# A two-layer decoder trunk: queries and keys multiplied with both parts of x^T in one operand, and the first attention's 1/rms moved into its tanh

## The chip, the cores and the metric

The kernel runs on one core of one Trainium2 chip. The metric is device time in microseconds for one execution of the whole program (two layers). PE is the matrix engine, ACT the scalar engine, DVE the vector engine, POOL the general one; SP issues the loads.

## The reference

The input x is 256 tokens by 1024. Both layers do the following, all in float32:

```python
h = _rmsnorm(x, g_mix)
proj = h @ w_in                     # q,k,v of three attentions, gates, an indexer
br_a = stick_breaking(qa, ka, va)   # 8 heads of 64, no positions
br_b = forgetting(qb, kb, vb)       # softmax with a forget bias
br_c = indexed_sparse(qc, kc, vc)   # top 64 keys for each query, by an indexer
y = sum(sigmoid(gate) * (br @ w_branch))
x = x + y @ w_out
x = x + relu(rmsnorm(x) @ w_up)**2 @ w_down
```

In the first attention, with z = q·k/8, a weight is sigmoid(z) times the product of 1 - sigmoid over the keys that lie between; the kernel takes sigmoid(z) from tanh(z/2).

## The kernel before

**Split operands.** Each float32 operand goes to PE as two parts, a rounded one ("hi") and the rest ("lo"), and a product is three matmuls: hi·hi, hi·lo, lo·hi (`mm3`, lines L119, L120, L121). The weights are split on the chip: a load brings 1 MB into `raw`, and for each half of it ACT copies the hi part (`whi`, L91) and DVE subtracts (`wlo`, L92, 128x1024). There are four buffers of `whi` and four of `wlo`, so the fifth half after a given one is not split before PE has done with that one. x^T stands in `xT` tiles that hold the hi and lo parts of two blocks of 128 features side by side; 1/rms of a token is not in it and is multiplied in later.

**One `feat`.** Queries and keys of the two attentions without positions are made by `feat`, eight times in each layer (`qa`, `ka`, `qb`, `kb`, two column groups each). A call takes 256 weight columns as two blocks b of 128. For each block and each of 8 blocks k of features there are three matmuls with the weights as the stationary operand and 256 columns of x^T moving; both blocks share one PSUM tile `mm`. DVE then multiplies the tile by `rb`, 1/rms laid along the tokens (L500, 128x512, `full`), and `q_stack` (ACT L145, DVE L147) or `k_stack` (ACT L153, L156, L157, DVE L155) splits `full` into the operands of the scores. There are three buffers of `mm` and four of the group "w3" that `full`, `e`, `th`, `m` and `R` share.

**Order of the work in a layer.** First the columns of the sparse attention, then `qa` and `ka` for two column groups, the values `va`, and beside them the indexer: its scores `sc` (L363 on ACT, L365 on DVE), then the search for the 64 best, 8 rounds of a maximum (L372) and a replacement (L373) on DVE for each 128 queries. Behind the values comes a first gate projection (its 8 k-blocks for one half of the tokens in a row, so that it takes four halves of weights in some 5 us), then the softmax of the sparse attention (`zc`, `e` L475, `pT` L440, `pTl` L444, `av` L456, `avs` L463) beside `qb` and `kb`, then the first attention (`za`, `th` L605, a scan `R` L617). The up projection of the feed-forward part, later in the layer, already moves both parts of x^T at once (`up_mm`, L686 with 512 columns, L687 with 256) and adds the halves (L674, L675).

Each engine runs its own instructions strictly in an order that a scheduler fixes when the program is built, from the dependences and its own estimate of times; so an edit in one place also shifts instructions of others.

Of the kernel before, what the change touches and what calls it, by code (L numbers as in the profile page):

```python
# [12 lines left out]
AF = mybir.ActivationFunctionType  # L13
OP = mybir.AluOpType

T, D, DEPTH, COLS, DFF = 256, 1024, 2, 7244, 4096
# [16 lines left out]
def trunk_kernel(ctx: ExitStack, tc: tile.TileContext, x, positions, g_mix, w_in, b_forget, w_branch,  # L33
                 w_out, g_mlp, w_up, w_down, g_final, out):
    nc = tc.nc
    act, dve, pool, pe, dma = nc.scalar, nc.vector, nc.gpsimd, nc.tensor, nc.sync
# [7 lines left out]
    def mm_tile(name="mm"):  # L44
        return ps.tile([128, 512], F32, name=name, tag="mm", bufs=3)
# [65 lines left out]
    def w_cols(src, off, rs):  # L111

        raw = raw_tile(8, 256)
        dma.dma_start(raw, AP(src, off, [[rs, 128], [128 * rs, 8], [1, 256]]))
        return [split(raw[:, :, 128 * b:128 * b + 128], 8, 128) for b in range(2)]

    def mm3(o, a, b, start, stop):
        (ah, al), (bh, bl) = a, b
        pe.matmul(o, ah, bh, start=start, stop=False)  # L119
        pe.matmul(o, ah, bl, start=False, stop=False)  # L120
        pe.matmul(o, al, bh, start=False, stop=stop)  # L121
# [9 lines left out]
    def blk(tiles, k, c0=0, c1=256, p0=0, p1=128):  # L131
        h, l = tiles[k // 2][:2]
        return h[p0:p1, k % 2, c0:c1], l[p0:p1, k % 2, c0:c1]
# [83 lines left out]
    for layer in range(DEPTH):  # L217
        wi0 = layer * D * COLS
        if layer == 0:
            wfirst = w_rows(w_in, C0 + 736, COLS, 0, 364, loads=4)  # L220
            load_x(1)
            xt, ss, part = norm_in(0, (at_tile, pt_tile))
# [3 lines left out]
        with tc.tile_pool(name=f"att{layer}", bufs=1, reuse_waits="tile") as att:  # L226
# [5 lines left out]
            rb = small.tile([128, 272], F32, name="rb", tag="rb", bufs=1)[:, 0:256]  # L232
            act.activation(rb, rp[:, 0:256], AF.Copy)

            rhalf = small.tile([128, 2], F32, name="rhalf", tag="rhalf", bufs=1)
# [101 lines left out]
            for n, c in enumerate((KI, KC, KC + 64)):  # L337
# [3 lines left out]
                p = at_tile("kT")  # L341
# [15 lines left out]
            for j, c, n in SEG:  # L357
                for h in range(4):
                    z = at_tile("zi")
                    i = h % 2  # L360
# [71 lines left out]
            ctok = small.tile([128, 2, NH], F32, name="ctok", tag="ctok", bufs=1)  # L432
            dve.tensor_copy(ctok, p[:, 0:16].rearrange("p (j h) -> p j h", j=2))


            def p_parts(e, i, scale):

# [52 lines left out]
                                           op0=OP.mult, op1=OP.mult)  # L490
                return e

            def feat(off, cp, is_q):

                o = mm_tile()
                for b, (h, l) in enumerate(w_cols(w_in, wi0 + off + cp * 256, COLS)):
                    for k in range(8):
                        mm3(o[:, b * 256:b * 256 + 256], (h[:, k, :], l[:, k, :]), blk(xt, k), k == 0, k == 7)
                full = work.tile([128, 2, 256], F32, name="full", tag="w3", bufs=4)
                dve.tensor_mul(full, o.rearrange("p (b t) -> p b t", b=2), rb.unsqueeze(1).to_broadcast([128, 2, 256]))  # L500
                if is_q:
                    q = stacked("qs")
                    q_stack(q, full, 0.125)
                    return q
                kt = stacked("ks")
                lo = att.tile([128, 2, 2, 256], F32R, name="ksl", tag="q4", bufs=8)
                k_stack(kt, lo, full)
                return kt, lo
# [21 lines left out]

            qa, ka = [], []
            for cp in range(2):
                qa.append(feat(0, cp, True))
                ka.append(feat(512, cp, False))
            va = values(1024)


# [62 lines left out]
            for b in range(4):  # L600
                th = work.tile([128, 2, 384], F32, name="th", tag="w3", bufs=4)
                for i in range(2):
                    z = at_tile("za")
                    qk(z, qa, ka, b, i)
                    act.activation(th[:, i, :], z[:, 0:384], AF.Tanh, scale=0.5)  # L605
                for c in (0, 256):
                    v = th[:, :, c:c + 128]
                    pool.affine_select(v, v, [[0, 2], [-1, 128]], OP.is_gt, -1.0, base=0, channel_multiplier=1)

                m = work.tile([128, 768], F32, name="m", tag="w3", bufs=4)  # L610
                pool.tensor_scalar(m[:, 0:767], th.rearrange("p i s -> p (i s)")[:, 1:768], -0.5, 0.5,
                                   op0=OP.mult, op1=OP.add)
                m2 = m.rearrange("p (i s) -> p i s", i=2)
                pool.memset(m2[:, :, 127:128], 0.0)
                pool.memset(m2[:, :, 383:384], 0.0)
                R = work.tile([128, 768], F32, name="R", tag="w3", bufs=4)
                dve.tensor_tensor_scan(R[:, ::-1], m[:, ::-1], ends[:, ::-1], 0.0, op0=OP.mult, op1=OP.add)  # L617
                dve.scalar_tensor_tensor(R, th.rearrange("p i s -> p (i s)"), 1.0, R, op0=OP.add, op1=OP.mult)
                Rv = R.rearrange("p (i s) -> p i s", i=2)
                parts = [p_parts(Rv, i, 0.5) for i in range(2)]  # L620
                av_pair(parts, lambda i, s: va[:, s, 2 * b + i, :], blk(brA, b))
# [45 lines left out]
        with tc.tile_pool(name=f"mlp{layer}", bufs=1, reuse_waits="tile") as mlp:  # L667
# [11 lines left out]
                act.activation(hi, r3, AF.Copy)  # L679
                dve.tensor_sub(lo, r3, hi.bitcast(F32))  # L680

            def up_mm(o, wb, ks):

                h, l = wb
                for k in ks:
                    pe.matmul(o, h[:, k, :], xt[k // 2][2][:, :, k % 2, :], start=k == 0, stop=False)  # L686
                    pe.matmul(o[:, 256:512], l[:, k, :], blk(xt, k)[0], start=False, stop=k == 7)  # L687

            first = []
            for c in range(16):  # L690
                uT.append((mlp.tile([128, 2, 256], F32R, name=f"uh{c}"), mlp.tile([128, 2, 256], F32R, name=f"ul{c}")))
# [67 lines left out]
```

## Time and profile before

| | |
|---|---|
| median of 3 runs | 885.59 us (885.42 to 887.14) |
| the profiled execution: its time | 883.07 us |
| its span in the trace | 881.3 us |
| PE, DVE, ACT, POOL busy | 98%, 73%, 61%, 13% of the span |
| granted clock of PE, mean | 0.997 of full speed |
| from layer 0 to the same place of layer 1 | about 432 us |

A share of busy time is a mean over the whole span. Matmuls are pipelined: the duration shown for one is longer than the distance to the next, and it is the distance from start to start that fills the time. On DVE and ACT too the next instruction can start slightly before the end shown of the one ahead of it.

### The profile page before, as it was taken

How to read it: one execution, taken by the hardware profiler on the slowest of the kernel's cores; microseconds unless marked ns; L12 is line 12 of the kernel's file. 1: busy time of each engine (PE TensorE's matmuls, PEld its weight loads, DVE VectorE, ACT ScalarE, POOL GpSimd, SP SyncE). 2: the span in 40 equal slices, each digit the busy share in tenths (PEclk: the TensorE clock that was granted, in tenths of full speed). 3: DMA queues.
4: the chain of work that ended last, by engine and by line, in shares of the span. 5: the costliest groups of instructions: out<-in, count | busy, mean ns of one | idle time of the engine just before them, and what ended most of it. 6: DMA issues, size and time to landing. Idle time of an engine off the chain costs nothing.

```text
span 881.3 us, 12928 instructions
## 1 busy us (share of the span) xinstructions
PE 865.4 (98%) x4830; PEld 759.2 (86%) x4830; DVE 645.0 (73%) x1072; ACT 533.4 (61%) x902; POOL 114.3 (13%) x216
## 2 busy tenths in 40 slices
PE   7999999999999999999999999999999999999996
PEld 6998998888888888888899989988888888888884
DVE  5889787978767777545468987789777587775552
ACT  6766886676466555435366758677755665554432
POOL 2300422234001000000011014022610100000001
PEclk9999999999999999999999999999999999999998
DMA  8744544344565555555466363454246566555521
GB/s 295 246 144 144 191 145 144 128 158 145 191 191 166 179 187 190 190 195 185 148 201 202 131 202 133 144 186 131 97 161 220 185 191 192 191 191 191 191 97 48
DMA packets 102479, 150.91 MB, mean 171 GB/s; under 512 B 2928, under 2 KB 58256, under 8 KB 102416
## 3 DMA queue, kind: packets, MB, share of 16 engines
q1 hardware_dynamic: 102416, 150.08, 52.2%
q8 instruction: 38, 0.62, 0.3%
q14 instruction: 25, 0.20, 0.1%
HBM read 149.02 MB, written 1.05 MB: 170 GB/s over the span
## 4 chain that ended last, share of the span: by engine, by line
PE 92%; DVE 5%; ACT 1%; DMA 1%; issue 1%; SPq 0%; POOL 0%; POOLq 0%; ACTq 0%
PE mm L120 20%; PE mm L119 20%; PE mm L121 20%; PE mm L686 13%; PE mm L687 6%; PE av L456 2%; PE pT L440 2%; PE at L120 1%; PE at L121 1%; PE at L119 1%; DVE wlo L92 1%; DVE qs L147 1%; PE xtp L170 1%; ACT qs L145 1%; DMA x<-in_x_dram 1%
## 5 line engine op out<-in xcount | busy, mean ns | idle before, releaser
L92 DVE TENSOR_TENSOR wlo<-raw,whi 128x1024 fp32r<-128x1024 f32 (+3 forms) x289 | 347.9, 1207 | 167.9 <-ACT whi L91 165.8
L91 ACT ACTIVATE whi<-raw 128x1024 fp32r<-128x1024 f32 (+3 forms) x289 | 298.8, 1037 | 240.0 <-PE mm L121 135.9
L686 PE MATMUL mm<-xT,whi 128*128 128x512 f32 x496 | 173.3, 393 | 0.6 <-DVE ut L675 0.6
L687 PE MATMUL mm<-xT,wlo 128*128 128x256 f32 x496 | 139.0, 280 | 0.0
L120 PE MATMUL mm<-wlo,xT 128*128 128x512 f32 (+2 forms) x320 | 122.1, 382 | 0.5 <-DVE wlo L92 0.5
L121 PE MATMUL mm<-whi,xT 128*128 128x512 f32 (+2 forms) x320 | 121.1, 381 | 0.0
L119 PE MATMUL mm<-whi,xT 128*128 128x512 f32 (+2 forms) x320 | 118.5, 381 | 0.4 <-ACT xT L175 0.4
L686 PEld LDWEIGHTS mm<-xT,whi 128*128 128x128 f32 x496 | 92.8, 187 | 21.9 <-PE mm L687 1.1
L121 PE MATMUL mm<-whi,ul 128*128 128x512 f32 x256 | 99.7, 390 | 0.0
L120 PE MATMUL mm<-wlo,uh 128*128 128x512 f32 x256 | 99.7, 389 | 0.0
L119 PE MATMUL mm<-whi,uh 128*128 128x512 f32 x256 | 98.9, 389 | 0.0
L687 PEld LDWEIGHTS mm<-xT,wlo 128*128 128x128 f32 x496 | 93.7, 189 | 0.1
L121 PE MATMUL mm<-xT,wlo 128*128 128x256 f32 x256 | 73.6, 287 | 0.0
L119 PE MATMUL mm<-xT,whi 128*128 128x256 f32 x256 | 73.2, 286 | 0.0
L120 PE MATMUL mm<-xT,whi 128*128 128x256 f32 x256 | 73.2, 286 | 0.0
L120 PEld LDWEIGHTS mm<-wlo,xT 128*128 128x128 f32 x320 | 60.4, 189 | 10.4 <-DVE wlo L92 1.4
L119 PEld LDWEIGHTS mm<-whi,xT 128*128 128x128 f32 x320 | 60.3, 189 | 10.3 <-ACT xT L175 0.8
L121 PEld LDWEIGHTS mm<-whi,xT 128*128 128x128 f32 x320 | 60.3, 189 | 9.1
L187 POOL TENSOR_TENSOR ms<-ss 128x2 f32<-128x2 f32 (+1 forms) x6 | 4.3, 718 | 469.4 <-ACT junk L180 295.2
L119 PEld LDWEIGHTS mm<-whi,uh 128*128 128x128 f32 x256 | 48.1, 188 | 10.0
L121 PEld LDWEIGHTS mm<-whi,ul 128*128 128x128 f32 x256 | 48.0, 188 | 10.0
L120 PEld LDWEIGHTS mm<-wlo,uh 128*128 128x128 f32 x256 | 48.1, 188 | 9.8
(218 smaller groups left out, 1487.9 us busy)
## 6 DMA issues: line engine op xcount, KB each, us to landing
raw<-in_w_in_dram SPq DMA_DIRECT2D x48, 1024.0 KB, 5.0
raw<-in_w_up_dram SPq DMA_DIRECT2D x32, 1024.0 KB, 5.1
raw<-in_w_down_dram SPq DMA_DIRECT2D x32, 1024.0 KB, 4.9
raw<-in_w_branch_dram SPq DMA_DIRECT2D x12, 1024.0 KB, 4.9
raw<-in_w_out_dram SPq DMA_DIRECT2D x8, 1024.0 KB, 4.9
raw<-in_w_in_dram SPq DMA_DIRECT2D x8, 736.0 KB, 5.2
raw<-in_w_in_dram SPq DMA_DIRECT2D x3, 728.0 KB, 4.3
out_dram<-x SPq DMA_DIRECT2D x4, 256.0 KB, 2.2
```

What stands on the lines that cost most here:

```text
L91: act.activation(h3[:, i:i + m], raw[:, i:i + m], AF.Copy)
L92: dve.tensor_sub(l3[:, i:i + m], raw[:, i:i + m], h3[:, i:i + m].bitcast(F32))
L119: pe.matmul(o, ah, bh, start=start, stop=False)
L120: pe.matmul(o, ah, bl, start=False, stop=False)
L121: pe.matmul(o, al, bh, start=False, stop=stop)
L145: act.activation(dst[half(i), :, i, :], src[half(i)], AF.Copy, scale=scale)
L147: dve.scalar_tensor_tensor(dst[half(1 - i), :, i, :], src[half(i)], scale, dst[half(i), :, i, :].bitcast(F32), op0=OP.mult, op1=OP.subtract)
L170: pe.transpose(p[:, i * 256 + j * 128:i * 256 + j * 128 + 128], xs[j][h][:, c:c + 128], ident)
L440: pe.transpose(p[:, q * 128:q * 128 + 128], e[:, i, q * 128:q * 128 + 128], ident)
L456: pe.matmul(o[:, c + c0:c + 256], v, p[:, a:b], start=s == 0 and n == 0, stop=s == 1 and n == 1)
L686: pe.matmul(o, h[:, k, :], xt[k // 2][2][:, :, k % 2, :], start=k == 0, stop=False)
L687: pe.matmul(o[:, 256:512], l[:, k, :], blk(xt, k)[0], start=False, stop=k == 7)
```

## The change

`feat` gets two switches. With `wide`, each block b has a PSUM tile of its own, and each k takes two matmuls: the hi weights against hi and lo of x^T side by side (512 columns, L439), and the lo weights against hi (256 columns, L440), added into the second half of the tile. ACT copies the second half to `full` (L509), and DVE adds the first half (L510). With `scaled`, DVE multiplies by 1/rms as before (L519). `qa` is wide and not scaled; `ka` is scaled and not wide, as before; `qb` and `kb` are both. Since `qa` now lacks its 1/rms, the tanh of the first attention multiplies by `rhalf` (half of 1/rms of the query's token, which is a row there); it is cut in two, for the two 128-query parts. `up_mm` is only moved up in the file.

```diff
+            def up_mm(o, wb, ks):
+
+                h, l = wb
+                for k in ks:
+                    pe.matmul(o, h[:, k, :], xt[k // 2][2][:, :, k % 2, :], start=k == 0, stop=False)
+                    pe.matmul(o[:, 256:512], l[:, k, :], blk(xt, k)[0], start=False, stop=k == 7)
...
-            def feat(off, cp, is_q):
-
-                o = mm_tile()
-                for b, (h, l) in enumerate(w_cols(w_in, wi0 + off + cp * 256, COLS)):
-                    for k in range(8):
-                        mm3(o[:, b * 256:b * 256 + 256], (h[:, k, :], l[:, k, :]), blk(xt, k), k == 0, k == 7)
+            def feat(off, cp, is_q, wide=True, scaled=True):
+
+
                 full = work.tile([128, 2, 256], F32, name="full", tag="w3", bufs=4)
-                dve.tensor_mul(full, o.rearrange("p (b t) -> p b t", b=2), rb.unsqueeze(1).to_broadcast([128, 2, 256]))
+                ws = w_cols(w_in, wi0 + off + cp * 256, COLS)
+                if wide:
+                    for b, (h, l) in enumerate(ws):
+                        o = mm_tile()
+                        up_mm(o, (h, l), range(8))
+                        act.activation(full[:, b], o[:, 256:512], AF.Copy)
+                        dve.tensor_add(full[:, b], o[:, 0:256], full[:, b])
+                    src = full
+                else:
...
+                if scaled:
+                    dve.tensor_mul(full, src, rb.unsqueeze(1).to_broadcast([128, 2, 256]))
...
-                qa.append(feat(0, cp, True))
-                ka.append(feat(512, cp, False))
+                qa.append(feat(0, cp, True, scaled=False))
+                ka.append(feat(512, cp, False, wide=False))
...
-                    act.activation(th[:, i, :], z[:, 0:384], AF.Tanh, scale=0.5)
+                    for j, c, n in SEG:
+                        act.activation(th[:, i, c:c + n], z[:, c:c + n], AF.Tanh, scale=rhalf[:, j:j + 1])
```

Numbers behind an underscore below are the program's own numbers of tiles; a tile that both programs have may carry different ones.

**First place: PE at the first `qa` block of layer 0.** Before, three matmuls of 256 columns for each k:

```order
L119 MATMUL mm_665<-xT_103,whi_668 128x256
L120 MATMUL mm_665<-xT_103,whi_668 128x256
L121 MATMUL mm_665<-xT_103,wlo_669 128x256
L119 MATMUL mm_665<-xT_103,whi_668 128x256
L120 MATMUL mm_665<-xT_103,whi_668 128x256
L121 MATMUL mm_665<-xT_103,wlo_669 128x256
L119 MATMUL mm_665<-xT_104,whi_668 128x256
L120 MATMUL mm_665<-xT_104,whi_668 128x256
L121 MATMUL mm_665<-xT_104,wlo_669 128x256
```
With the change, two for each k, of 512 and 256 columns:

```order
L439 MATMUL mm_676<-xT_103,whi_668 128x512
L440 MATMUL mm_676<-xT_103,wlo_669 128x256
L439 MATMUL mm_676<-xT_103,whi_668 128x512
L440 MATMUL mm_676<-xT_103,wlo_669 128x256
L439 MATMUL mm_676<-xT_104,whi_668 128x512
L440 MATMUL mm_676<-xT_104,wlo_669 128x256
```
What moved: nine instructions have become six, with as many moving columns.

**Second place: DVE in layer 0, behind the values' last weights.** Before: `wlo_983` are the last weights of `va`, `wlo_1271` the first of the gate behind it; `qs` and `ksl` are the split queries and keys, `sc` and `m8` the search:

```order
L147 SCALAR_TENSOR_TENSOR qs_726<-full_724,qs_726 64x2x256
L155 TENSOR_TENSOR ksl_793<-full_790,ks_792 64x2x256 x2
L373 MATCH_REPLACE sc_492<-m8_559,sc_492 128x128
L92 TENSOR_TENSOR wlo_983<-raw_976,whi_982 128x1024
L147 SCALAR_TENSOR_TENSOR qs_863<-full_861,qs_863 64x2x256 x2
L372 MAX m8_562<-sc_492 128x8
L372 MAX m8_565<-sc_492 128x8
L92 TENSOR_TENSOR wlo_1271<-raw_1268,whi_1270 128x1024
L433 COPY ctok_663<-cumt_659 128x16
L423 CAST crow_654<-chi_652 128x256
L373 MATCH_REPLACE sc_492<-m8_562,sc_492 128x128
```
With the change the last weights of `va` are `wlo_959` (six rows further up), and `wlo_1247` and `wlo_1251` are the first two halves of the gate:

```order
L92 TENSOR_TENSOR wlo_1247<-raw_1244,whi_1246 128x1024
L373 MATCH_REPLACE sc_492<-m8_553,sc_492 128x128
L372 MAX m8_556<-sc_492 128x8
L373 MATCH_REPLACE sc_492<-m8_556,sc_492 128x128
L372 MAX m8_559<-sc_492 128x8
L373 MATCH_REPLACE sc_492<-m8_559,sc_492 128x128
L147 SCALAR_TENSOR_TENSOR qs_612<-ctT_607,qs_612 64x2x256 x2
L372 MAX m8_562<-sc_492 128x8
L372 MAX m8_565<-sc_492 128x8
L147 SCALAR_TENSOR_TENSOR qs_714<-full_665,qs_714 64x2x256 x2
L155 TENSOR_TENSOR ksl_781<-full_719,ks_780 64x2x256
L373 MATCH_REPLACE sc_492<-m8_562,sc_492 128x128
```
What moved: rounds of the search that stood ahead of the values' weights now stand between the gate's weights. From behind the third of the four halves of `va` to the last half of the gate, in layer 0, DVE has 7 replacements of 128 columns where it had 3, 6 maxima of 128 where it had 3, 3 score rows L365 of 256 columns where it had none, one cast less (L427), and all else alike; PE has six more matmuls (`zi`, 256 columns). In layer 1 the same stretch has 5 and 5 of the 128-column steps, one step less of each kind of 256, 2 score rows, and four more `zi`.

**Third place: PE and DVE in layer 1, in the sparse attention's softmax.** Before, PE behind the last scores `zc` of the stage; the rows go on with matmuls of `kb`, 53 of them in all before the first use of `pTl_5434`:

```order
L350 MATMUL zc_5527<-kl_4785,qs_4929 128x256
L456 MATMUL av_5384<-pTl_5381,vc_4934 128x256
L456 MATMUL av_5384<-pTh_5380,vc_4934 128x128
L456 MATMUL av_5384<-pTl_5381,vc_4934 128x128
L119 MATMUL mm_5795<-xT_3920,whi_5798 128x256
L120 MATMUL mm_5795<-xT_3920,whi_5798 128x256
L440 MATMUL pT_5429<-ident_76,e_5410 128x128
L121 MATMUL mm_5795<-xT_3920,wlo_5799 128x256
L119 MATMUL mm_5795<-xT_3920,whi_5798 128x256
L120 MATMUL mm_5795<-xT_3920,whi_5798 128x256
```
DVE before, in the same place, up to that `pTl`:

```order
L155 TENSOR_TENSOR ksl_5247<-full_5244,ks_5246 64x2x256 x2
L475 ISA e_5532,mx_5533<-zc_5527,mb_4906 128x128
L475 ISA mx_5533 128x1
L475 ISA e_5532,mx_5533<-zc_5527,mb_4906 128x256
L475 ISA mx_5533 128x1
L92 TENSOR_TENSOR wlo_5874<-raw_5867,whi_5873 128x1024
L463 TENSOR_TENSOR avs_5393<-av_5384,avs_5393 64x256 x2
L500 TENSOR_TENSOR full_5788<-mm_5729,rb_4532 128x512
L444 SCALAR_TENSOR_TENSOR pTl_5434<-pT_5429,pTh_5433 128x384
```
With the change PE has there, behind `zc_5443`, the transposes and eight matmuls of the first attention's scores (`za`), and then at once the matmuls that need `pTl_5350`:

```order
L447 MATMUL pT_5345<-ident_76,e_5326 128x128 x2
L447 MATMUL pT_5353<-ident_76,e_5326 128x128 x3
L349 MATMUL za_5957<-ks_5037,qs_4971 128x128
L350 MATMUL za_5957<-ksl_5038,qs_4971 128x128
L349 MATMUL za_5957<-ks_5037,qs_4971 128x256
L350 MATMUL za_5957<-ksl_5038,qs_4971 128x256
L349 MATMUL za_5964<-ks_5037,qs_4971 128x128
L350 MATMUL za_5964<-ksl_5038,qs_4971 128x128
L349 MATMUL za_5964<-ks_5037,qs_4971 128x256
L350 MATMUL za_5964<-ksl_5038,qs_4971 128x256
L463 MATMUL av_5361<-pTh_5349,vc_4874 128x256
L463 MATMUL av_5361<-pTl_5350,vc_4874 128x256
```
DVE with the change:

```order
L155 TENSOR_TENSOR ksl_5163<-full_5101,ks_5162 64x2x256 x2
L493 RECIPROCAL rs_5391<-sm_5389 128x4
L482 ISA e_5448,mx_5449<-zc_5443,mb_4846 128x128
L482 ISA mx_5449 128x1
L482 ISA e_5448,mx_5449<-zc_5443,mb_4846 128x256
L482 ISA mx_5449 128x1
L92 TENSOR_TENSOR wlo_5819<-raw_5816,whi_5818 128x1024
L470 TENSOR_TENSOR avs_5309<-av_5300,avs_5309 64x256 x2
L451 SCALAR_TENSOR_TENSOR pTl_5350<-pT_5345,pTh_5349 128x384
L451 SCALAR_TENSOR_TENSOR pTl_5358<-pT_5353,pTh_5357 128x384
```
What moved: the first attention's scores come earlier, and 53 matmuls of `kb` no longer lie between the last scores of the stage and the first use of the `pTl` that stands behind them on DVE.

## Rows read from the trace of the kernel before

**Rows 1.** The page: busy time by engine, and the chain that ended last by engine.

```profile
PE 865.4 (98%) x4830; PEld 759.2 (86%) x4830; DVE 645.0 (73%) x1072; ACT 533.4 (61%) x902; POOL 114.3 (13%) x216
...
PE 92%; DVE 5%; ACT 1%; DMA 1%; issue 1%; SPq 0%; POOL 0%; POOLq 0%; ACTq 0%
```

**Rows 2.** What PE waited for: us in total, times, longest.

```profile
PE av L456 <- DVE pTl L444: 0.6, 2, 0.3
...
PE mm L120 <- DVE wlo L92: 0.5, 2, 0.3
```

**Rows 3.** Timeline of PE, inside a block of `feat`: start, duration (us), instruction.

```profile
38.64 0.28 PE L119 MATMUL mm<-xT,whi 128*128 128x256 f32 x1
...
39.00 0.28 PE L119 MATMUL mm<-xT,whi 128*128 128x256 f32 x1
```

**Rows 4.** Timeline of PE, the up projection.

```profile
299.91 0.39 PE L686 MATMUL mm<-xT,whi 128*128 128x512 f32 x1
...
305.81 0.39 PE L686 MATMUL mm<-xT,whi 128*128 128x512 f32 x1
```

**Rows 5.** DVE by line and shape: count, busy us, mean ns of one, idle before.

```profile
L92 DVE TENSOR_TENSOR wlo<-raw,whi 128x1024 fp32r<-128x1024 f32 x264 | 325.9, 1237 | 152.3 <-ACT whi L91 150.5
L675 DVE TENSOR_TENSOR ut<-mm,ut 128x256 f32<-128x256 f32 x62 | 25.8, 418 | 0.0
...
L444 DVE SCALAR_TENSOR_TENSOR pTl<-pT,pTh 128x384 fp32r<-128x384 f32 x48 | 25.3, 551 | 1.0 <-ACT pTh L443 0.7
L463 DVE TENSOR_TENSOR avs<-av,avs 64x256 f32<-64x256 f32 x48 | 20.1, 419 | 7.8 <-ACT avs L461 7.4
...
L155 DVE TENSOR_TENSOR ksl<-full,ks 64x512 fp32r<-64x512 f32 x16 | 11.5, 719 | 0.8 <-PE zc L349 0.4
L500 DVE TENSOR_TENSOR full<-mm,rb 128x512 f32<-128x512 f32 x16 | 11.0, 687 | 0.3
...
L475 DVE CUSTOM_DVE_ANT_0 e<-zc,mb 128x256 f32<-128x256 f32 x16 | 6.6, 420 | 0.0
...
L372 DVE MAX8 m<-sc 128x8 f32<-128x128 f32 x16 | 4.7, 293 | 0.3
...
L373 DVE MATCH_REPLACE8 sc<-m,sc 128x128 f32<-128x128 f32 x16 | 4.4, 278 | 0.0
L475 DVE CUSTOM_DVE_ANT_0 e<-zc,mb 128x128 f32<-128x128 f32 x16 | 4.4, 287 | 0.5 <-POOL mb L377 0.4
...
L365 DVE SCALAR_TENSOR_TENSOR sc<-ri,wh,sc 128x256 f32<-128x256 f32 x6 | 2.8, 472 | 0.0
L373 DVE MATCH_VALUE_LOAD sc<-m,sc 128x8 f32 x32 | 2.8, 88 | 0.5
```

**Rows 6.** ACT by line and shape, the same columns.

```profile
L674 ACT ACTIVATE ut<-mm 128x256 f32<-128x256 f32 x62 | 22.3, 363 | 0.0
...
L605 ACT ACTIVATE th<-za 128x384 f32<-128x384 f32 x16 | 7.2, 487 | 9.0 <-DVE R L617 4.5 <-PE za L350 4.4
```

**Rows 7.** Timeline of DVE, the end of `va` and the gate, layer 0.

```profile
59.00 1.23 DVE L92 TENSOR_TENSOR wlo<-raw,whi 128x1024 fp32r<-128x1024 f32 x1 [0.29 <-ACT whi L91]
...
78.25 1.22 DVE L92 TENSOR_TENSOR wlo<-raw,whi 128x1024 fp32r<-128x1024 f32 x1
```

**Rows 8.** Timeline of PE, the gate's last weights, layer 0.

```profile
78.64 0.39 PE L121 MATMUL mm<-whi,xT 128*128 128x512 f32 x1
78.87 0.39 PE L119 MATMUL mm<-whi,xT 128*128 128x512 f32 x1
79.52 0.50 PE L120 MATMUL mm<-wlo,xT 128*128 128x512 f32 x1 [0.26 <-DVE wlo L92]
```

**Rows 9.** Timeline of PE, eight score matmuls and the next instruction.

```profile
96.70 0.22 PE L349 MATMUL zc<-kh,qs 128*128 128x128 f32 x1
...
97.61 0.40 PE L120 MATMUL mm<-wlo,xT 128*128 128x512 f32 x1
```

**Rows 10.** Window 100 to 131 us: busy (count) of PE, PEld, DVE, ACT, POOL; clock; DMA.

```profile
100.00:131.00 31.00, 31.00 (x257) 30.72 (x256) 26.43 (x55) 27.43 (x62) 10.14 (x15) 1.00 0.42 137
```

More of the change, by code (lines that the diff above doesn't have):

```diff
@@ L491, in softmax_pair @@
                 return e
-            def feat(off, cp, is_q):
-                o = mm_tile()
-                for b, (h, l) in enumerate(w_cols(w_in, wi0 + off + cp * 256, COLS)):
-                    for k in range(8):
-                        mm3(o[:, b * 256:b * 256 + 256], (h[:, k, :], l[:, k, :]), blk(xt, k), k == 0, k == 7)
-                full = work.tile([128, 2, 256], F32, name="full", tag="w3", bufs=4)
-                dve.tensor_mul(full, o.rearrange("p (b t) -> p b t", b=2), rb.unsqueeze(1).to_broadcast([128, 2, 256]))
+            def feat(off, cp, is_q, wide=True, scaled=True):
+                full = work.tile([128, 2, 256], F32, name="full", tag="w3", bufs=4)
+                ws = w_cols(w_in, wi0 + off + cp * 256, COLS)
[7 more added lines that the diff above has]
+                else:
+                    o = mm_tile()
+                    for b, (h, l) in enumerate(ws):
+                        for k in range(8):
+                            mm3(o[:, b * 256:b * 256 + 256], (h[:, k, :], l[:, k, :]), blk(xt, k), k == 0, k == 7)
+                    src = o.rearrange("p (b t) -> p b t", b=2)
+                if scaled:
+                    dve.tensor_mul(full, src, rb.unsqueeze(1).to_broadcast([128, 2, 256]))
                 if is_q:
@@ L680, in up_done @@
                 dve.tensor_sub(lo, r3, hi.bitcast(F32))
[L682 to L687, printed above, removed]
             first = []
```

## The prediction

> **What bounds the kernel now.** I read the page first. PE is busy for 98% of the span, and the chain that ended last runs through PE for 92% of it [rows 1]; the clock is granted in full where it is listed [rows 10]. So the time is the sum of the distances between matmuls, plus what PE waits. The list of PE's waits is next: inside the layers it has hardly any, 0.5 to 0.6 us in two pieces each [rows 2]. Two consequences. What the change takes from PE's own work is saved, unless a wait takes its place; and there is almost no wait left that the change could remove, but many that it could create, since DVE is busy for 73% of the span and ACT for 61%. So the third look is at the places where PE waits already. The `wlo` wait is at the last weights of the first gate: PE starts a matmul at 78.87 and the next, which needs them, at 79.52 instead of 0.23 later (78.64 to 78.87), 0.42 us late [rows 8]. They were made from 78.25 to 79.47 [rows 7], and DVE had no idle time between the end of the `wlo` that starts at 59.00 and this one: 19.24 us of queue. Of that stretch PE has nothing to spare; it will show every DVE instruction that is put into it. The second such place is the softmax beside `qb` and `kb`: from 100 to 131 us ACT is busy 27.43 of 31 us and DVE 26.43 [rows 10], while PE never stops.
>
> **The change on PE.** For each k of a block three matmuls become two, with the same columns. Three take 0.36 us (38.64 to 39.00) [rows 3]. The pair has run in the up projection: 17 of them from 299.91 to 305.81, 0.347 us each [rows 4]. That is 0.013 us less. Six of the eight `feat` calls in a layer are wide, so 6 calls x 2 blocks x 8 k x 2 layers = 192 groups: 2.5 us. The starts are printed to 0.01 us, so 0.36 may be 0.355 to 0.365, and the gain 1.5 to 3.5 us; I take 2.5. No gain at all is excluded by these rows, since both forms ran here, on operands of the same kind. A rule weighed against this: the Trainium skill, "TensorE: Matmul & The Clock Gate", section "Wait — 56ns, not 53.3ns?", gives a warm matmul a fixed cost of about 2.5 ns beyond its columns. By that figure the 192 matmuls less would give only 0.5 us, and the whole sum would end 2 us higher; the rows show 13 ns for each, and the sum goes by them.
>
> **The change on ACT and DVE, by work.** Each of the 24 wide blocks adds an ACT copy and a DVE add, both seen in the up projection at 0.363 and 0.418 us [rows 5, 6]: 8.7 and 10.0 us in all. Four multiplications of `qa` go, at 0.687 [rows 5]: 2.7 us. With `qb` and `kb` the multiplication now reads SBUF rather than PSUM; no row shows it, and I keep 0.687 (at best it falls to that of an add of half the size, 0.42; at worst it takes two of them, 0.84; 8 of them change 2 us of DVE's work either way, none of it in the stretch of [rows 7]). The tanh: 16 of 0.487 become 32; the second one costs ACT between nothing and another 0.363 each, 0 to 5.8 us, in a stage where ACT waited 9.0 us ahead of this line [rows 6]: nothing for PE. Behind PE's saving there is thus more work of the helpers, some 4 to 7 us for each layer on either engine, and over the whole run there are gaps enough; what counts is which queues it lengthens.
>
> **First wait: the gate behind the values.** The order shows that the helper work of `qa` pushes rounds of the indexer's search to later places: in layer 0, between the third half of `va`'s weights and the last half of the gate's, DVE has four replacements of 128 columns more (0.278 and a load of 0.088 each), three maxima (0.293) and three score rows (0.472) [rows 5]: 1.46 + 0.88 + 1.42 = 3.8 us, less a small cast, which I put at 0.2 by estimate: 3.5. PE gets six `zi` matmuls more in the same stretch, at 0.114 (eight such from 96.70 to 97.61) [rows 9]: 0.7. The stretch starts on both sides at the same event, since the third half can be split only when PE has left the `ka` block whose buffer it takes. As DVE is already 0.42 late there, all of the difference shows: 2.8 us. Bounds: nothing if ACT's or the load's lateness was what set DVE in this stretch (then DVE would have shown idle time, it shows 0.29 at the start only), 3.5 if PE's `zi` are hidden. In layer 1 the same count is 2 x (0.366 + 0.293 + 0.472) = 2.3, less one maximum and one replacement of 256 columns and the cast (1.1, estimated from the 128-column rows times 1.4, and 0.2), less 4 `zi` (0.5): 0.7. What is behind the late `wlo` on DVE is the rest of the search, for which nobody waits yet. Together 3.5.
>
> **Second wait: `pTl_5350` in layer 1.** From the end of the scores `zc_5438` DVE has, until this `pTl` is there: two pairs of `e` (0.42 + 0.287 each), `ksl` twice (0.719), a `wlo` (1.237), `avs` twice (0.419) and the `pTl` (0.551) [rows 5]: 5.5 us. PE has 27 small matmuls in that time (`av`, `zc`, `pT`, `za`): at 0.114, 3.1 us [rows 9]. So PE would wait 2.4 us. Before, 53 matmuls of `kb`, at 0.12 [rows 3], stood in between, 6 us more, and PE waited for nothing. Bounds: 0, if `ksl` and the first pair are through earlier than I count; 2.4. I take 2.2, since DVE starts an instruction slightly before the shown end of the one ahead. Behind it stand `pTl_5358` (0.551) and the add that frees a PSUM tile for the next `kb` block (0.418), 1.0 us, while PE has 13 small matmuls, 1.5 us: no third wait there.
>
> **Sum.** -2.5 + 3.5 + 2.2 = +3.2 us. The profiled execution took 883.07, its span 881.3; the median of the runs is 885.59, 2.5 above it. The change is put on the median: 888.8 us, where a profiled execution would show about 886.3.
>
> **The rivals.** *Faster.* The queues catch up: in the stage of `qa` DVE's own work rises by only 4 x 0.418 - 2 x 0.687 = 0.3 us per layer, and the search that stands later could find DVE free later. Then both waits stay where they were, at tenths, and 2.5 us are saved: 883.1. For it speaks that DVE idled for 152 us ahead of `wlo` over the run [rows 5], against it that none of this idle time lies in the stretch of [rows 7]. It decides if DVE enters the gate's stretch more than 3 us ahead. The Trainium skill, "Perfetto Trace Analysis", section "Identifying the Most-Contended Engine", would have the engine of highest occupancy improved first, which PE is here; by that rule alone the time is this rival's. *No change.* One of the two places costs what I count, the other little: -2.5 + 2.2 to 3.5 = about 0 to +1, 885.3 to 886.6. *Slower still.* From 100 to 131 us ACT gets 8 copies per layer, 2.9 us on 27.4 of 31 [rows 6, 10], and the tanh of the first attention now falls into the same time with `za` moved up. Above 31 the scan `R` and the transposes behind it come late too: 2 us a layer, 892.8.
>
> **How the numbers follow.** A measurement of this kernel can tell about 0.2%, 1.8 us, from no change. My forecast, 887.4 to 890.5, has a chance of 0.36, the slower rival 0.17, so slower 0.53; no change 0.27; faster 0.20. The forecast's time is the likeliest: 888.8. The range reaches down to the faster rival's upper part, 883.5, and up to 892.0, leaving about 0.15 below and 0.05 above.
>
> **What the new profile would show.** Right: L439 and L440 at a pair pitch of 0.347; a wait of PE for `wlo` of some 3 us around 79 us and of 1 us at the same place of layer 1; a wait for `pTl` of 2 us near the end of the sparse attention in layer 1; PE's busy time 2 to 3 us lower. Wrong: PE's waits as short as before, or long waits at other names (`full`, `whi`, `R`, a PSUM tile held by the new adds), or a pair in `feat` slower than in the up projection.

## The result and the profile after

The changed kernel takes **897.4 us** (895.97 to 898.52, 4 runs) against 885.5 us (883.97 to 887.14, 4 runs) in the same comparison: a ratio of 1.0125, 95% interval [1.011, 1.0139]. It is slower, as forecast, but by 11.9 us instead of 3.2, and outside the range.

First two lines of the page of the changed kernel (busy time by engine; the chain that ended last), which answer to [rows 1]:

```profile
PE 870.6 (97%) x4638; PEld 750.9 (84%) x4638; DVE 653.0 (73%) x1092; ACT 542.4 (61%) x942; POOL 115.1 (13%) x216
...
PE 85%; DVE 9%; issue 2%; ACT 2%; POOL 1%; DMA 1%; SPq 0%; POOLq 0%; DVEq 0%; ACTq 0%
```

And its list of what PE waited for (us in total, times, longest), which answers to [rows 2]:

```profile
PE mm L120 <- DVE wlo L92: 4.6, 5, 1.2
...
PE za L349 <- DVE mx L482: 1.8, 2, 1.4
PE pT L447 <- DVE R L638: 1.7, 2, 1.2
PE av L463 <- ACT full L509: 1.3, 1, 1.3
PE mm L439 <- DVE ut L695: 0.6, 2, 0.3
PE zc L349 <- DVE ctok L433: 0.4, 1, 0.4
```

The chain has gone from 92% PE to 85%, and the waits inside the layers from some 2 us to over 10, under names that hardly waited before: weights (`wlo`), scores (`za`), the scan's transposes (`pT`), a value matmul (`av`). The idle time in this list is counted from the modelled end of the matmul ahead; the distance from start to start, less the usual one, is longer, and it is what the span pays. By that measure:

| place | layer 0 | layer 1 | before |
|---|---|---|---|
| gate behind the values (78 to 83, 520 us) | 2.4 | 1.1 | 0.4 each |
| softmax of the sparse attention (116 to 117, 552 to 554 us) | 2.3 | 2.4 | about 0 |
| scan R and its transposes (146, 603 us) | 1.3 | 0.8 | 0 |
| weights and values behind the next R (172, 608 to 611 us) | 1.3 | 1.9 | 0 |

That is 12.7 us more than before, less what the pairs save. From the first `rp` matmul at a layer's start to the first `xtp` transpose behind its attentions, layer 0 grew by 6.45 us (244.82 to 251.27) and layer 1 by 4.67 (244.36 to 249.03), 11.1 together. The table less 2.1 us of saving gives 10.6; two waits of 0.5 us at `av` that the kernel before had (199 and 631 us) are gone as well, so some 1.5 us lie in pieces that the table doesn't list. The two profiled spans differ by 13.8 us, and the other 2.7 lie outside these stretches: the work ahead of the first `rp` ended 1.3 us later (15.34 against 14.03; from 13.6 to 15.9 in the traces of this case), and the up projection of layer 1 took 1.3 us more (last section).

The gate, forecast from [rows 7, 8]: the timeline of PE in the changed kernel (start, duration, instruction, idle before it):

```profile
79.58 0.50 PE L120 MATMUL mm<-wlo,xT 128*128 128x512 f32 x1 [0.40 <-DVE wlo L92]
...
81.71 0.28 PE L350 MATMUL zc<-kl,qs 128*128 128x256 f32 x1
82.91 0.50 PE L120 MATMUL mm<-wlo,xT 128*128 128x512 f32 x1 [0.92 <-DVE wlo L92]
```

and of DVE, the last `wlo` of that gate:

```profile
81.64 1.21 DVE L92 TENSOR_TENSOR wlo<-raw,whi 128x1024 fp32r<-128x1024 f32 x1
```

The last weights are ready at 82.85 and PE, whose last score matmul started at 81.71, goes on at 82.91, 1.2 us later, where 0.1 is usual. Two more waits stand ahead of it on the same queue (the weights at 79.58, and at 78.45 a score that waits for the copy `ctok`).

The pair in `feat`, in the timeline of PE of the changed kernel, which answers to [rows 3, 4]:

```profile
40.48 0.39 PE L439 MATMUL mm<-xT,whi 128*128 128x512 f32 x1
...
41.89 0.40 PE L439 MATMUL mm<-xT,whi 128*128 128x512 f32 x1
```

Four pairs in 1.41 us, 0.353; the median of the 155 undisturbed ones in `feat` is 0.349. Against 0.360 for three matmuls that is 0.011 us less, 2.1 us for 192.

The softmax in layer 0, by the changed kernel's chain that ended last (start, duration, what); this wait was not in the forecast's sum:

```profile
112.13 1.55 ACT e L491 x7
113.70 0.18 DVE rs L493
113.88 0.57 DVE ksl L155
114.48 0.75 DVE ksl L155
...
115.56 0.14 DVE e L482
...
115.91 0.33 DVE avs L470
...
116.71 0.57 DVE pTl L451
117.32 0.73 PE av L463 x4
```

DVE's reciprocal for a later tile waits for ACT's exponentials until 113.7; the timeline of DVE shows the idle time before it:

```profile
113.70 0.18 DVE L493 RECIPROCAL rs<-sm 128x4 f32<-128x4 f32 x1 [1.82 <-ACT e L491]
```

Behind it in the strict order stand `ksl`, the maxima of `e`, `avs` and `pTl`, which PE wants at once. None of them is long; the one that waits at the head holds the others.

In layer 1 nothing waits at the head. The timeline of DVE there:

```profile
549.07 0.29 DVE L482 CUSTOM_DVE_ANT_0 e<-zc,mb 128x128 f32<-128x128 f32 x1 [0.34 <-PE zc L350]
...
551.69 1.25 DVE L92 TENSOR_TENSOR wlo<-raw,whi 128x1024 fp32r<-128x1024 f32 x1
552.86 0.85 DVE L470 TENSOR_TENSOR avs<-av,avs 64x256 f32<-64x256 f32 x2
553.74 1.02 DVE L451 SCALAR_TENSOR_TENSOR pTl<-pT,pTh 128x384 fp32r<-128x384 f32 x2
```

From the end of the scores DVE works without idle time until the first `pTl` is there at 554.3: 5.2 us, the queue that the forecast counted.

The first attention has the pattern of layer 0 one stage later, in the chain again:

```profile
165.90 1.71 POOL m L631
...
167.83 1.76 DVE R L637
...
170.35 0.86 DVE R L638
171.22 1.15 DVE wlo L92
...
172.41 0.50 PE mm L120
```

The weights that PE needs at 171 are split behind a scan that itself waits for POOL (0.94 us of idle time on DVE). The transposes of R at 146 us are late for another reason: the chain ahead of them is DVE's queue, with no gap above 0.1 us from 136.2 to 145.8.

### The profile page after: what moved, and what is told of

Read it like the earlier page. It is cut to its first block, busy times and chain, and to the rows that moved or that the text cites. A ratio compares the mean times of both kernels' runs of the same rounds, so it can differ in the third digit from the quotient of the medians.

```text
span 895.1 us, 12621 instructions
## 1 busy us (share of the span) xinstructions
PE 870.6 (97%) x4638; PEld 750.9 (84%) x4638; DVE 653.0 (73%) x1092; ACT 542.4 (61%) x942; POOL 115.1 (13%) x216
## 4 chain that ended last, share of the span: by engine, by line
PE 85%; DVE 9%; issue 2%; ACT 2%; POOL 1%; DMA 1%; SPq 0%; POOLq 0%; DVEq 0%; ACTq 0%
PE mm L439 17%; PE mm L120 16%; PE mm L119 16%; PE mm L121 16%; PE mm L440 9%; DVE wlo L92 3%; PE av L463 2%; PE pT L447 1%; PE at L120 1%; PE at L121 1%; PE at L119 1%; DVE ksl L155 1%; DVE qs L147 1%; DVE R L637 1%; PE xtp L170 1%
## 5 line engine op out<-in xcount | busy, mean ns | idle before, releaser
L92 DVE TENSOR_TENSOR wlo<-raw,whi 128x1024 fp32r<-128x1024 f32 (+3 forms) x289 | 350.9, 1217 | 184.6 <-ACT whi L91 182.5
L439 PE MATMUL mm<-xT,whi 128*128 128x512 f32 x688 | 244.4, 398 | 0.6 <-DVE ut L695 0.6
L440 PE MATMUL mm<-xT,wlo 128*128 128x256 f32 x688 | 193.6, 281 | 0.0
L439 PEld LDWEIGHTS mm<-xT,whi 128*128 128x128 f32 x688 | 129.1, 188 | 30.3 <-PE mm L440 1.1
L440 PEld LDWEIGHTS mm<-xT,wlo 128*128 128x128 f32 x688 | 130.0, 189 | 0.2
L119 PE MATMUL mm<-whi,xT 128*128 128x512 f32 (+2 forms) x320 | 121.5, 385 | 0.4 <-ACT xT L175 0.4
L121 PE MATMUL mm<-whi,xT 128*128 128x512 f32 (+2 forms) x320 | 121.0, 382 | 0.0
L496 POOL TENSOR_SCALAR e<-e,rs 128x128 f32<-128x128 f32 x64 | 37.3, 600 | 38.0 <-DVE rs L493 35.7
L119 PE MATMUL mm<-whi,k2h 128*128 128x512 f32 x96 | 37.8, 394 | 0.0
L120 PE MATMUL mm<-wlo,k2h 128*128 128x512 f32 x96 | 37.4, 390 | 0.0
```

The lines of the kernel that those rows point to most:

```text
L92: dve.tensor_sub(l3[:, i:i + m], raw[:, i:i + m], h3[:, i:i + m].bitcast(F32))
L496: pool.tensor_scalar(e[:, i, c:c + n], e[:, i, c:c + n], rs[:, i, j:j + 1], 1.0, op0=OP.mult, op1=OP.mult)
```

## The experiments

Several explanations were put up against each other. Theory A: the new work on ACT and DVE (copies, adds, the second tanh) lengthens their queues. Theory B, later E: the wide form costs by itself, by a PSUM tile for each block. Theory C: the cut tanh. Theory D, later F: the order of instructions that the scheduler chose. Theory G, the rival of F: the parts' work together is too much for ACT and DVE in any order. "Before" is run beside each on the same chip.

**e1_qa_only.** `qb` and `kb` narrow as before.

```diff
-                qb.append(feat(1536, cp, True))
-                kb.append(feat(2048, cp, False))
+                qb.append(feat(1536, cp, True, wide=False))
+                kb.append(feat(2048, cp, False, wide=False))
```

> Only the queries of the first attention are wide and unscaled (with the tanh cut in two); qb and kb are as before. Theory A (the helper engines' queues are lengthened by the copies and adds, and PE pays where it then waits): the gate's late weights come back, +2 to +3 us in layer 0 and +0.5 in layer 1, less 0.6 us of PE's saving, so 887 to 889; the wait in the sparse attention's softmax, which sits beside qb and kb, stays away. Theory B (the wide form with its own PSUM tile for each block costs PE itself, whatever the helpers do): a third of the loss, 889 to 890, spread over the qa blocks and not at named waits. Theory C (the cut tanh and the unscaled queries carry the loss): 895 or more.

891.96 us, ratio 1.0061 [1.0044, 1.0079]: between the ranges, no theory gave it. The gate's waits are there as in the change (0.68 and 1.20 us from start to start), the softmax's are not; but layer 1 has new ones of 1.9, 0.7 and 0.6 us (for `y`, `k2h` and `v`), which nothing of the edit explains.

**e2_qbkb_only.** `qa` and the tanh as before.

```diff
-                qa.append(feat(0, cp, True, scaled=False))
+                qa.append(feat(0, cp, True, wide=False))
...
-                    for j, c, n in SEG:
-                        act.activation(th[:, i, c:c + n], z[:, c:c + n], AF.Tanh, scale=rhalf[:, j:j + 1])
+                    act.activation(th[:, i, :], z[:, 0:384], AF.Tanh, scale=0.5)
```

> Only qb and kb are wide; qa and the tanh are as before. Theory A: no late gate weights beyond the 0.4 us of before; the waits for the softmax's scores and transposes (2.3 us in layer 0, 2.4 in layer 1) and for the late scan R come, less 1.2 us of saving: 891 to 894. Theory B: two thirds of the loss, 893. Theory C: the time of before less the saving, 884 to 885.

891.41 us, 1.0053 [1.0034, 1.0072], in theory A's range. No late gate beyond that of before, 2.0 us in each softmax and 0.9 at each R, as theory A says.

**e4_pe_only.** The wide matmuls without the helpers' new work; the second half of each tile is left out.

```diff
-                        act.activation(full[:, b], o[:, 256:512], AF.Copy)
-                        dve.tensor_add(full[:, b], o[:, 0:256], full[:, b])
-                    src = full
+                        dve.tensor_mul(full[:, b], o[:, 0:256], rb)
+                    src = None
...
-                qa.append(feat(0, cp, True, scaled=False))
+                qa.append(feat(0, cp, True))
...
```

> All of qa, qb, kb have the two wide matmuls, but the second half of the tile is neither copied nor added, so the products with the low part of x^T and of the weights are left out of the result; DVE multiplies the first half by 1/rms, and the tanh is one instruction as before. PE does exactly the matmuls of the change, the helpers as much as before. Theory A: PE's saving is seen, 192 pairs at 0.007 to 0.013 us, 883 to 885, and no waits beyond those of before. Theory B: slower than before by most of the 12 us.

893.94 us, 1.0082 [1.0065, 1.0099]. Theory A fails here: without a single copy or add, most of the loss is there, at the gate and in the softmax, and at places of its own. Its list of PE's waits:

```profile
PE mm L120 <- DVE wlo L92: 3.5, 3, 1.7
PE mm L119 <- DVE y L584: 1.5, 2, 0.8
PE mm L119 <- DVE v L538: 1.4, 2, 0.7
PE av L463 <- ACT ksl L157: 1.3, 1, 1.3
```

**e5_helpers_only.** The helpers' work with three matmuls of 256 columns, a PSUM tile for each block.

```diff
-                        up_mm(o, (h, l), range(8))
-                        act.activation(full[:, b], o[:, 256:512], AF.Copy)
+                        for k in range(8):
+                            mm3(o[:, 0:256], (h[:, k, :], l[:, k, :]), blk(xt, k), k == 0, k == 7)
+                        act.activation(full[:, b], o[:, 0:256], AF.Copy, scale=0.0)
```

> The helpers' work of the change with the matmuls of before: three of 256 columns for each k, one PSUM tile for each block; ACT copies the block with a factor of zero, DVE adds it, so that the result is the same; the tanh is cut in two. Theory A: the waits of the changed kernel without its saving on PE, 897 to 900. Theory B: near before, 886 to 888.

895.29 us, 1.0103 [1.0078, 1.0127]: below theory A's range and far above B's, and not with A's waits. The gate waits nearly as little as before (0.56 us), the softmax some 0.7; 2.5 us a layer are lost at a wait for `y`, which the changed kernel does not have.

**e3_tanh_only.** Nothing wide; `qa` unscaled, split straight from PSUM.

```diff
                 if scaled:
                     dve.tensor_mul(full, src, rb.unsqueeze(1).to_broadcast([128, 2, 256]))
+                else:
+                    full = src
...
-                qa.append(feat(0, cp, True, scaled=False))
+                qa.append(feat(0, cp, True, wide=False, scaled=False))
...
```

> No wide matmuls at all: qa is unscaled, q_stack reads its PSUM tile directly (no copy to full, four DVE multiplications less), and the tanh is cut in two. Theory C of the earlier runs (the cut tanh carries the loss) would give 893 or more. Theory A (work and place of the helpers' instructions): DVE's queue in the gate's stretch is 1.0 us longer in each layer by the order's count, nothing else changes: 886 to 889.

892.39 us, 1.0073 [1.0048, 1.0097]; a miss for A, and short of C's. It waits for `th` (1.4 a layer) and `qs` (1.2 a layer).

**f1_pin_za, f2_pin_za_qs.** The changed kernel with edges that fix only the issue order: the first scores of the first attention behind the last matmul of `kb`; in f2 also the splits of `qa` and the first `ka` behind the gate's last weights.

```diff
+                    if b == 0:
+                        with tc.issue_after(kbend.ins):
+                            qk(z, qa, ka, b, i)
...
```

> The changed kernel with one edit of the order: the first two score tiles of the first attention (za, 16 matmuls) may not be issued on PE before the last matmul of kb, as they stood before the change. No work is added or removed. Theory D (the order that the scheduler chose, not the amount of work, makes the waits in the softmax): the waits for scores and transposes there go (2.3 and 2.4 us), the gate's stay, 891 to 894. Theory A (the copies and adds themselves are too much for that stage): 896 to 898, as the changed kernel.

> As the one before, and besides the splits of qa and of the first ka (DVE, six instructions, 4.2 us in each layer) may not be issued before the gate's last weight split, so that DVE's queue in the gate's stretch is 2.4 us shorter in layer 0 and 1.7 in layer 1. Theory D: the late gate weights go too (1.8 us and 0.5 us), 889 to 892. Theory A: 895 to 898.

898.41 us, 1.0141 [1.0106, 1.0176], and 898.42, 1.0139 [1.011, 1.0169]. Neither gains, and theory D's ranges are missed. In f2 the gate's weights are late by only 0.65 us in layer 0 and not at all in layer 1, but other waits now stand there: 1.0 us for the gate's own instruction on ACT (L581) in layer 0, and 1.7 us in layer 1 for the values' on DVE (`v`, L543), which stands behind the splits that were held back. In both kernels PE waits some 3 us at one value matmul in each layer: DVE's queue is as late as ever, and the scores that used to fill the hole are gone. So my single cause for that wait (the scores moved ahead) was wrong. What the longer hole adds stands in the windows of f1 (columns as in [rows 10]):

```profile
108.00:114.00 6.00, 6.00 (x44) 5.54 (x43) 3.88 (x10) 4.15 (x12) 3.86 (x5) 1.00 0.52 165
117.30:120.00 2.70, 2.70 (x12) 2.46 (x13) 2.70 (x6) 2.67 (x8) 0.00 (x0) 0.50 0.00 0
123.50:126.00 2.50, 2.50 (x15) 2.15 (x15) 1.73 (x4) 1.65 (x3) 0.00 (x0) 1.00 0.00 0
```

Behind the hole the granted clock is 0.50, the 1.2 GHz level, and the pairs take 0.64 us (121.06 to 121.70) until it is back.

**k2_psum_only.** The kernel before with a PSUM tile for each block.

```diff
+                    d = mm_tile()[:, 0:256] if own else o[:, b * 256:b * 256 + 256]
                     for k in range(8):
-                        mm3(o[:, b * 256:b * 256 + 256], (h[:, k, :], l[:, k, :]), blk(xt, k), k == 0, k == 7)
+                        mm3(d, (h[:, k, :], l[:, k, :]), blk(xt, k), k == 0, k == 7)
+                    if own:
+                        dve.tensor_mul(full[:, b], d, rb)
```

> The kernel before with one edit: each of the two blocks of qa, qb and kb has a PSUM tile of its own, as in the change, and DVE multiplies each by 1/rms (two instructions of 256 columns for one of 512). Matmuls, ACT's work and the tanh are as before. Theory E (two PSUM tiles for each call, of three, hold PE back while the tile waits for a buffer of full, so that the first attention's scores are put into the hole and the softmax's queues come late): the waits of the softmax and of the scan R come back without any new work, 889 to 894. Theory A (the copies, adds and the second tanh carry the loss): 886 to 887.

886.09 us, 1.0009 [0.9997, 1.0022]: no loss. Theory E falls: a PSUM tile for each block costs nothing by itself.

**k3_work_only.** The copies and adds with the shared PSUM tile.

```diff
+                    for b in range(2):
+                        act.activation(full[:, b], o[:, b * 256:b * 256 + 256], AF.Copy, scale=0.0)
+                        dve.tensor_add(full[:, b], o[:, b * 256:b * 256 + 256], full[:, b])
```

> The kernel before with the helpers' new work alone: both blocks share a PSUM tile as before; ACT copies each block (with a factor of zero) and DVE adds it, then DVE multiplies as before: 24 copies and 24 adds more, nothing else. Theory E: the place of the first attention's scores stays, little is lost, 885 to 889. Theory A: 892 to 897.

884.44 us, 0.9989 [0.9975, 1.0003]: no loss. Theory A falls: alone, and in the order of this kernel, 24 copies and 24 adds are hidden.

**k1_after_full_own, k0_before_full_own.** `full` in four buffers of its own, three load buffers.

```diff
-                full = work.tile([128, 2, 256], F32, name="full", tag="w3", bufs=4)
+                full = work.tile([128, 2, 256], F32, name="full", tag="full", bufs=4)
...
-        raw = wp.tile([128, 2048], F32, name="raw", tag="raw", bufs=4)
+        raw = wp.tile([128, 2048], F32, name="raw", tag="raw", bufs=3)
```

> The changed kernel, with four buffers of its own for full (it shared four with e, th, m and R), so that a PSUM tile can be copied out as soon as it is complete; for the room the load buffers go from four to three. Theory E: the waits in the softmax fall by half or more, the gate's late weights stay, 889 to 894. Theory A: 896 to 898.

> Control for the one before: the kernel before with the same four buffers of its own for full and three load buffers. Both theories: within 1.5 us of the kernel before, 884 to 887; if three load buffers cost, it shows here.

901.66 us, 1.018 [1.0157, 1.0203], and 890.1, 1.0049 [1.0028, 1.007]; both outside what was expected. The control is 4.5 us slower (three load buffers, or the new place of the others; not told apart), and more buffers for `full` give nothing. Inconclusive beyond that.

**m1_change_in_good_order, m2_old_work_in_changed_order.** Parts that cost nothing alone (k2, k3) and others that cost 7 us alone (e3) do not add up; what is left as common to the slow builds is that they are other orders. So the order was set by hand: a table of indices for each engine, taken from k2's schedule for the change's work, and from the changed kernel's schedule for k2's work.

```diff
...
+        for a, b in zip(idx, idx[1:]):
+            tc.add_manual_dep(own[b], own[a].name, nosync, reason="order")
...
         trunk_kernel(tc, *args)
+        in_order(tc)
```

> All of the change's work (wide matmuls, copies, adds, the cut tanh), but each engine issues in the order of k2_psum_only, the kernel with before's work and a PSUM tile for each block that took 886.1: a table of indices fixes it, with the pair in the place of the three matmuls, each add in the place of its multiplication, each copy ahead of it, the second tanh behind the first. Theory F (the order that the scheduler chose for the changed program makes the loss, and the work itself is hidden): 883 to 888, no wait at the gate beyond 0.5 us. Theory G (the work of the parts together is too much for ACT and DVE in whatever order): 892 to 898.

> The reverse: the work of k2_psum_only (before's matmuls, no copies, no adds, one tanh; 886.1 in its own order), but each engine issues in the order of the changed kernel. Theory F: most of the loss is there without the work, 892 to 899, with the late gate weights and the softmax's waits at the same places. Theory G: 885 to 888.

m1: 888.24 us, 1.0031 [1.002, 1.0042]. m2: 897.06 us, 1.0129 [1.011, 1.0148]. This decides it: old work in the changed kernel's order takes the changed kernel's time, and the change's work in k2's order loses 2.6 us instead of 11.9 (0.2 us above what theory F gave, and with 0.9 us of waiting at the gate where F gave 0.5 at most). What PE waited for in m2:

```profile
PE mm L145 <- DVE wlo L117: 4.1, 5, 1.0
PE za L374 <- DVE mx L500: 1.6, 2, 1.2
PE av L481 <- DVE avs L488: 1.3, 1, 1.3
```

The same places as in the changed kernel, and nearly the same sizes. Distances from start to start at the late instruction:

| place | changed kernel | m2 |
|---|---|---|
| gate, layer 0 | 0.68, 1.20 | 0.68, 1.20 |
| gate, layer 1 | 1.20 | 1.20 |
| softmax, layer 0 | 1.70, 0.42, 0.50 | 1.50, 0.41, 0.50 |
| softmax, layer 1 | 0.70, 1.58, 0.50 | 0.70, 1.58, 0.50 |
| weights behind R | 1.57, 1.52 | 1.17, 1.43 |
| transposes of R | 1.55, 0.92 | 0.49, none |

Of these only the transposes of R are much shorter without the work. One thing that the times hold is not in this table. In m2's profiled execution the granted clock is 0.50, the 1.2 GHz level, behind the softmax's waits; its windows (columns as in [rows 10]):

```profile
117.00:120.30 3.30, 3.30 (x18) 3.30 (x18) 3.06 (x8) 3.24 (x13) 1.02 (x3) 0.50 0.00 0
554.00:560.60 6.60, 6.60 (x30) 6.36 (x31) 5.74 (x14) 5.35 (x16) 2.12 (x6) 0.50 0.00 1
```

In the changed kernel's profiled execution it is 1.00 in both stretches. A matmul of 256 columns takes 0.21 us there instead of 0.12, near 5 us in all by an estimate from these distances. In this execution m2's two layers are 14.6 us longer than those of the kernel before, some 9 of them waits by distance. So the order alone costs some 9 us in waits, and the lower clock behind them comes on top. The execution of m2 with a mean clock of 0.998 took 896.28 us, that of the changed kernel with the same mean clock 896.79.

Now m1, its list of PE's waits:

```profile
PE mm L145 <- DVE wlo L117: 1.4, 2, 0.7
...
PE pT L472 <- DVE R L663: 0.9, 2, 0.5
PE pT L472 <- DVE pTl L476: 0.8, 2, 0.4
```

and its window from 100 to 131 us (columns as in [rows 10]):

```profile
100.00:131.00 31.00, 30.18 (x194) 26.44 (x193) 26.20 (x58) 29.74 (x72) 10.85 (x16) 1.00 0.30 103
```

Here ACT is busy 29.74 of 31 us (27.43 before, [rows 10]); PE gives back in short waits what the pairs save, and 2.6 us more. That the copies on a full ACT are the reason fits, but was not tested apart.

**n1_change_old_tanh, n2_helpers_old_tanh.** The change, and e5, with `qa` scaled and one tanh instruction.

```diff
-                qa.append(feat(0, cp, True, scaled=False))
+                qa.append(feat(0, cp, True))
...
-                    for j, c, n in SEG:
-                        act.activation(th[:, i, c:c + n], z[:, c:c + n], AF.Tanh, scale=rhalf[:, j:j + 1])
+                    act.activation(th[:, i, :], z[:, 0:384], AF.Tanh, scale=0.5)
```

> The change with qa scaled by DVE as before and one tanh instruction: wide matmuls, copies and adds only. If the tanh carries a part of its own (7 us when made alone), 888 to 891; if each edit only brings another order (theory F), anything from 888 to 898, with the gate's late weights of 2 us in layer 0, which its order shows, and nothing to be added up from the parts.

> Before's matmuls with a PSUM tile for each block, the copies and the adds, and the old tanh: the sum of k2_psum_only and k3_work_only, which both took the time of before. If parts add up: 884 to 887. If the two together are too much for the helpers (theory G): 892 or more.

895.36 us, 1.0112 [1.0092, 1.0132], and 886.49, 1.0016 [1.0003, 1.0028]. k2's and k3's parts together cost 0.9 us. With the cut tanh and unscaled `qa` (e5) the same kernel loses 8.4 (895.29 against 886.9 beside it), while taking these two out of the change gains 2.0 us at most (895.36 against 897.4, from different comparisons; their intervals overlap). So the cut tanh with unscaled `qa` has no fixed price: about 7 us in two pairs of orders that the scheduler chose (e3 against before, e5 against n2), 2.0 or less in another, and in m1, where the order is held, all of the change's work, the tanh among it, costs 2.6.

## Why the prediction was wrong, step by step

- **PE's saving.** Right in kind; 0.011 us for each group (0.349 against 0.360) instead of 0.013: 2.1 us instead of 2.5. The fixed cost of about 2.5 ns for each matmul, which the Trainium skill gives ("TensorE: Matmul & The Clock Gate", "Wait — 56ns, not 53.3ns?"), would have made 0.5 us, by an estimate from it; the traces don't agree, and the measured distances decide. One sign of being right did not come: PE's busy time did not fall by 2 to 3 us, it is 870.6 against 865.4. It counts each matmul to its modelled end, and the saving shows in the distances alone.
- **First wait, the gate.** Right in place and nearly in size: by distances 2.0 and 0.7 us more than before, against 2.8 and 0.7. Its reason was wrong, though. The prediction put it on "the helper work of `qa`", but with all the helper work but narrow matmuls (e5, n2) the order keeps 3 or 4 replacements and 3 maxima in that stretch of layer 0, and the gate waits 0.56 us; with wide matmuls and no helper work (e4) there are 6 and 6, and PE waits 2.9 us there in layer 0 and 1.1 in layer 1. From the third half of `va`'s weights to the last of the gate's, DVE's queue in layer 0 takes 22.4 to 22.7 us in each build with a wide `qa` (the change, e1, e4, n1), and the late gate is in all of them; with a narrow `qa`, in an order of the scheduler's own, it takes 18.7 to 20.0. In m2, which has narrow matmuls in the changed kernel's order, it is 22.4 as well. So the reading of the order held, and what it was put down to did not.
- **Second wait, `pTl` in layer 1.** Right in size (2.4 us, at three matmuls, against 2.2) and in mechanism: DVE's queue took 5.2 us against 5.5 counted. Wrong as the only one: the same stage of layer 0 lost 2.3 us, which the sum left out, and there it is the reciprocal at the head that waits, behind POOL and ACT. That the scores were moved ahead was not the cause in either layer: keeping them back (f1, f2) made the hole longer.
- **The rival "slower still"** put a late R, 2 us a layer, on top of the forecast: 888.8 + 4 = 892.8. The range ended at 892.0, below this rival's own time, although the rival had a chance of 0.17. R's transposes did come late, but by 2.1 us in both layers together, and behind R came 3.2 us more for the weights and values that stand behind it on DVE, which no case had. The rival's reason did not hold: ACT was to need more than 31 us of the window from 100 to 131, and in the changed kernel it is busy 28.40 (columns as in [rows 10]):

```profile
100.00:131.00 31.00, 29.30 (x193) 26.11 (x192) 25.29 (x62) 28.40 (x66) 11.03 (x19) 1.00 0.39 132
```

- **The step that failed is the sum.** "-2.5 + 3.5 + 2.2" prices two places that were counted, and puts every other place at nothing, without a count there: it assumes that everything else in a changed order waits as little as before. Four stages were late, not two: 12.7 us instead of 5.7. What the sum left out are the softmax of layer 0 (2.3), the transposes of R (2.1) and what stands behind R (3.2).
- **The faster rival** did not come: idle time of DVE over the whole run (184.6 us ahead of `wlo` even now) was no help in queues that are full for 20 us. What PE saves was real, and lost six times over; the rule to improve the engine of highest occupancy first (the Trainium skill, "Perfetto Trace Analysis", "Identifying the Most-Contended Engine") did not give the time here.

What stays open is why the scheduler's own estimates lead to a slower order in this change and in most of its parts (e1 to e5, n1); no trace shows them. And no version with the wide matmuls beats the kernel before: with 2.1 us at stake, m1 (888.24) is the nearest, and a better place for the copies on ACT was not tried.

## What to carry to other kernels

When a scheduler builds the order, an edit is two changes: the work, and a new order everywhere downstream. Price each stage whose order is new, add the late places up, and don't assume that a stage that did not wait before will not wait now. Better, hold the order fixed (a table of issue edges) to see what the work costs by itself, and run the old work in the new order to see what the order costs. On an engine that issues in order, look for the instruction at the head that waits (here a reciprocal, a scan), and for what the busiest engine wants behind it.

## What the hardware showed that was not expected

The same pair in the up projection runs at one of two steady distances, and which one changes from layer to layer and from trace to trace. In the timeline of PE of the kernel before, layer 1, the first and the last of 33 starts (32 pairs):

```profile
732.65 0.39 PE L686 MATMUL mm<-xT,whi 128*128 128x512 f32 x1
...
743.75 0.39 PE L686 MATMUL mm<-xT,whi 128*128 128x512 f32 x1
```

and of the changed kernel, the same stretch:

```profile
744.68 0.40 PE L439 MATMUL mm<-xT,whi 128*128 128x512 f32 x1
...
755.98 0.40 PE L439 MATMUL mm<-xT,whi 128*128 128x512 f32 x1
```

11.10 us against 11.30, 0.347 and 0.353 for a pair, at the same granted clock. In the 17 traces of this case the mean of a layer's pairs is always near one of these two (0.347 to 0.348, or 0.353). It doesn't hang on the wide form of `feat`: k2, without it, has 0.353 in both layers. What sets it, no run shows; there is one trace of each kernel, so runs of the same kernel were not compared. Over the 248 pairs of a layer the difference is 1.5 us, by this rate; it accounts for 1.3 of the 13.8 us between the two profiled spans, and is nearly half of the spread of the runs (3.2 us for the kernel before).
